# A row sum of 64 MiB: the first two blocks get 17 and 15 rows for each partition, and each its own store

## The chip, the cores and the metric

The kernel runs on one core of a Trainium2 chip. The metric is the device time of one execution in microseconds (us). A profiled execution also has a span, from its first to its last instruction; the time is about 1.8 us more than the span. Times carry noise of a few tenths of a microsecond.

## The reference

```python
# x: float32 [32, 512, 1024]
def reference(x):
    return np.sum(x, axis=-1).astype(np.float32)      # [32, 512]
```

There are 16384 rows of 1024 numbers (4 KiB each), and one sum for each row. With 128 partitions that is 128 rows for each partition, 67.1 MB to read and 64 KiB to write.

## The kernel before

The rows are taken in eight blocks of 16 rows for each partition. Partition p of a block reads 16 neighbouring rows, so neighbouring partitions begin 64 KiB apart in memory. Three buffers rotate. VectorE (DVE) sums whole blocks; ScalarE (ACT) helps in the last two.

```python
    x_g = x.flatten_outer_dims().rearrange("(g p j) d -> g p j d", p=P, j=BIG)     # BIG = 16
    out_v = out.rearrange("b s -> (b s)").rearrange("(g p j) -> p g j", p=P, j=BIG)
    ...
        for g in range(last):                                   # last = 7
            t = inpool.tile([P, BIG * dim + 4], fp32)           # bufs=3
            if g == 0:
                rows(t, 0, FIRST, 0, 0)                         # FIRST = 4: load 4 rows, sum them
                first = sums_of[-1]
                rows(t, FIRST, BIG - FIRST, FIRST, 0)           # load 12, sum them
                continue
            load = rows(t, 0, BIG, g * BIG, BIG // 2 if g == last - 1 else 0)
            ...
        # the last block comes in pieces of 8, 5, 2 rows and two parts of one row
        ...
        hold(store(nc.scalar, 0, last), two, "its packets come behind those of the loads")
        halves(whole[:, :1], part)
        halves(sums[:, j : j + 1], whole)                       # the last sum
        store(nc.sync, last, last + 1)
```

`rows` issues a load on SyncE's queue (SPq in the profile) and the reductions for it. The sums of blocks 0 to 6 leave in one store from ScalarE's queue (ACTq), held until the load `two` has landed (its completion is signalled to the waiting engine); the store writes 128 x 7 = 896 pieces of 16 sums, 64 bytes each. The sums of block 7 leave in a small store from SyncE's queue. Before the closing barrier SyncE waits, in what is called its drain here, for every load and for the ScalarE store. It does not wait there for the last store: GpSimd waits for that one, after the barrier, just before it clears the semaphores.

## Time and profile before

| | before |
|---|---|
| time, median of 3 | 161.64 us (161.48 to 161.78) |
| span of the profiled execution | 159.6 us |
| load queue, share of 16 DMA engines | 97.8% |
| VectorE busy | 120.1 us |
| first load lands | 7.14 us |
| last VectorE sum starts | 157.45 us |
| from there to the end | 2.15 us |

The first landing and the start of the last sum cut the span into a start, a middle and a tail. The prediction shows the lines.

The final store is the last thing in the chain. Its landing at 159.31 releases the clear, and the barrier is done before that. This gives the drain some slack, and one of the two arguments below is about how much.

### The profile page before, as it was taken

The numbers are of one execution on the slowest core, as the hardware profiler recorded it, in microseconds if no ns is written. First come the engines' busy times: TensorE is split into PE (matmuls) and PEld (weight loads), VectorE is DVE, ScalarE is ACT, GpSimd is POOL, SyncE is SP. The second block draws the span as 40 slices with busy tenths as digits, with TensorE's granted clock in tenths as the row PEclk, the third lists the DMA queues.
The fourth block names the chain that finished last, engine by engine and source line by source line (L and its number), as shares of the span: only waits on it lengthen the run. The fifth ranks groups of instructions, "written<-read, shape, count | busy, mean of one in ns | idle before, by whom it ended". The sixth has DMA issues, their size and how long they took to land.

```text
span 159.6 us, 125 instructions
## 1 busy us (share of the span) xinstructions
DVE 120.1 (75%) x22; ACT 17.3 (11%) x31; POOL 0.2 (0%) x4
## 2 busy tenths in 40 slices
DVE  0290059960799958999499994999949999497953
ACT  3000000000000000000000000000000000496953
POOL 0000000000000000000000000000000000000000
DMA  7999996996996989979969969969969969798984
GB/s 263 460 406 579 394 526 263 526 526 263 526 526 263 526 378 411 526 312 476 526 279 509 526 263 526 526 263 526 526 263 526 509 279 526 337 452 371 467 365 128
DMA packets 2928, 67.18 MB, mean 421 GB/s; under 512 B 1264, under 2 KB 1392, under 8 KB 1520
## 3 DMA queue, kind: packets, MB, share of 16 engines
q1 hardware_dynamic: 2016, 67.12, 97.8%
q10 hardware_dynamic: 912, 0.06, 0.4%
HBM read 67.11 MB, written 0.07 MB: 421 GB/s over the span
## 4 chain that ended last, share of the span: by engine, by line
DMA 73%; DVE 25%; SPq 1%; issue 0%; DVEq 0%
DMA t<-in_x_dram 73%; DVE sums L141 24%; SPq L180 1%; SPq L221 0%; DVE t L155 0%; DVEq L252 0%
## 5 line engine op out<-in xcount | busy, mean ns | idle before, releaser
L141 DVE TENSOR_REDUCE sums<-t 128x16 f32<-128x16384 f32 (+3 forms) x9 | 116.6, 12954 | 35.3 <-DMA t<-in_x_dram 35.3
L168 ACT ACTIVATE unread<-t 128x1024 f32<-128x1024 f32 x15 | 15.2, 1012 | 139.2 <-DMA t<-in_x_dram 139.2
L155 DVE CUSTOM_DVE_ANT_0 t<-t 128x512 f32<-128x512 f32 (+2 forms) x6 | 3.5, 602 | 2.4 <-DMA t<-in_x_dram 2.4
L168 ACT ACTIVATION_READ_ACCUMULATOR unread<-t 128x1 f32 x15 | 2.8, 187 | 0.0
L168 ACT ACT_TABLE_LOAD x1 | 1.3, 1283 | 0.8 <-PEq L241 0.8
L155 DVE DVE_READ_ACCUMULATOR2_ANT sums<- 128x1 f32 x5 | 0.4, 83 | 0.0
L241 POOL MEMSET const-uint8-127<- 128x1 uint8 x1 | 0.1, 102 | 0.0
L241 POOL MEMSET const-bfloat16-1.0<- 128x1 bf16 x1 | 0.1, 101 | 0.0
L241 POOL MEMSET const-float32-0.0<- 128x1 f32 x1 | 0.1, 98 | 0.2 <-issue 0.2
L241 POOL MEMSET const-float32-1.0<- 128x1 f32 x1 | 0.1, 98 | 0.0
L155 DVE DVE_READ_ACCUMULATOR2_ANT t<- 128x1 f32 x1 | 0.1, 81 | 0.0
L219 DVE MEMSET t<- 128x1 f32 x1 | 0.1, 59 | 0.0
## 6 DMA issues: line engine op xcount, KB each, us to landing
t<-in_x_dram SPq DMA_DIRECT2D x1, 6144.0 KB, 20.9
t<-in_x_dram SPq DMA_DIRECT2D x1, 4096.0 KB, 31.1
t<-in_x_dram SPq DMA_DIRECT2D x1, 2560.0 KB, 36.9
t<-in_x_dram SPq DMA_DIRECT2D x1, 2048.0 KB, 7.1
t<-in_x_dram SPq DMA_DIRECT2D x1, 1024.0 KB, 38.9
t<-in_x_dram SPq DMA_DIRECT2D x1, 280.0 KB, 39.1
t<-in_x_dram SPq DMA_DIRECT2D x1, 232.0 KB, 39.2
t<-in_x_dram SPq DMA_DIRECT2D x6, 40.8
```

Source lines behind the costliest of these rows:

```text
L141: return nc.vector.tensor_reduce(out=dst, in_=src, axis=mybir.AxisListType.X, op=mybir.AluOpType.add)
L155: return nc.vector.tensor_tensor_reduce(out=src[:, :n], in0=src[:, :n], in1=src[:, n:], scale=1.0, scalar=0.0, op0=mybir.AluOpType.add, op ...
L168: nc.scalar.activation(out=unread[:, :n], in_=src, func=mybir.ActivationFunctionType.Copy, accum_out=dst,)
L180: load = nc.sync.dma_start(out=block, in_=rows_from(j, n))
L219: nc.vector.memset(whole[:, width + 1 :], 0.0)
L241: nc = _bacc.Bacc("TRN2", target_bir_lowering=False, num_devices=1)
```

## The change

The change gives block 0 seventeen rows for each partition and block 1 fifteen. Partitions of block 0 are then 68 KiB apart in memory, not 64. No stated reason came with it; breaking up a power-of-two distance when all engines start together is the likely one. One access pattern no longer describes the outputs of blocks 0 and 1, so each gets its own store. ScalarE now issues three stores where it issued one.

```diff
+    sizes = [BIG + 1, BIG - 1] + [BIG] * (J // BIG - 2)
+    begins = [sum(sizes[:k]) for k in range(len(sizes))]
+    x_b = [
+        x_r[a * P : (a + n) * P].rearrange("(p j) d -> p j d", p=P) for a, n in zip(begins, sizes)
+    ]
+    out_b = [out_r[a * P : (a + n) * P].rearrange("(p j) -> p j", p=P) for a, n in zip(begins, sizes)]
+    out_g = out_r[2 * BIG * P :].rearrange("(g p j) -> p g j", p=P, j=BIG)
     ...
         for g in range(last):
-            t = inpool.tile([P, BIG * dim + 4], fp32)
+            n, j = sizes[g], begins[g]
+            t = inpool.tile([P, (BIG + 1) * dim], fp32)
     ...
-        hold(store(nc.scalar, 0, last), two, "its packets come behind those of the loads")
+        for k in range(2):
+            mine = sums[:, begins[k] : begins[k] + sizes[k]]
+            hold(nc.scalar.dma_start(out=out_b[k], in_=mine), two, behind)
+        middle = sums[:, 2 * BIG : last * BIG].rearrange("p (g j) -> p g j", j=BIG)
+        hold(nc.scalar.dma_start(out=out_g[:, : last - 2], in_=middle), two, behind)
     ...
-        store(nc.sync, last, last + 1)
+        nc.sync.dma_start(out=out_b[last], in_=sums[:, last * BIG :])
```

## The prediction

> **What bounds the kernel now.** I read four views: the page's busy shares and queue table, the merged chain of waits, the timeline of VectorE (DVE), and the stretches of time.
>
> ```profile
> DVE 120.1 (75%) x22; ACT 17.3 (11%) x31; POOL 0.2 (0%) x4
> q1 hardware_dynamic: 2016, 67.12, 97.8%
> ```
>
> VectorE has work for 120.1 of 159.6 us. The load queue's packets cover 97.8% of the span on all 16 DMA engines. The transfers have next to no room.
>
> ```profile
> 7.17 4.42 DVE L141 TENSOR_REDUCE sums<-t 128x4 f32<-128x4096 f32 x1 [7.17 <-DMA t<-in_x_dram]
> 21.67 12.95 DVE L141 TENSOR_REDUCE sums<-t 128x12 f32<-128x12288 f32 x1 [10.08 <-DMA t<-in_x_dram]
> 41.02 17.22 DVE L141 TENSOR_REDUCE sums<-t 128x16 f32<-128x16384 f32 x1 [6.39 <-DMA t<-in_x_dram]
> 60.37 17.22 DVE L141 TENSOR_REDUCE sums<-t 128x16 f32<-128x16384 f32 x1 [2.14 <-DMA t<-in_x_dram]
> 79.76 17.22 DVE L141 TENSOR_REDUCE sums<-t 128x16 f32<-128x16384 f32 x1 [2.17 <-DMA t<-in_x_dram]
> ```
>
> Columns: start, duration, instruction, idle time before it with its releaser. Blocks land every 19.35 us (60.37 - 41.02) and a reduction takes 17.22, so VectorE waits 2.1 us for data at every block. A block is 8.39 MB, so the rate is 8.39/19.35 = 434 GB/s. One row for each partition costs 19.35/16 = 1.209 us of transfer and 17.22/16 = 1.076 us of VectorE.
>
> ```profile
> 0.00:7.14 7.14, 0.00 (x0) 1.28 (x1) 0.20 (x4) 1.00 1.02 404
> 7.14:157.45 150.31, 119.67 (x20) 16.03 (x30) 0.00 (x0) 1.00 0.99 427
> 157.45:159.60 2.15, 0.41 (x2) 0.00 (x0) 0.00 (x0) 1.00 0.18 18
> ```
>
> Columns: stretch, its length, busy time of VectorE, ScalarE and GpSimd, clock, DMA share, GB/s. I cut the span where the first load lands and where the last VectorE sum starts. The middle carries 124 of the 128 rows: 124 x 1.209 = 149.96 of its 150.31 us. It can lose 0.35 us and no more. The first stretch carries 4 rows, 4.84 us of data, in 7.14: 2.3 us are start-up. The last is 2.15 us of a sum, a small store and the closing barrier. So a change in block sizes can act at the two ends only.
>
> **What the Trainium skill says.** "DMA: Bandwidth & Descriptors", section "Bandwidth", "Where 436 GB/s comes from", puts the ceiling at 435 GB/s; the 434 above agrees, so the middle is at it. The same page, "Latency and other measured facts", tells of copies slowing where the row pitch between partitions is a large power of two: 207 GB/s at 512 KiB, 103 at 4 MiB, back to 214 when 4 KiB are added to the pitch. Here a block of 16 rows has a pitch of 64 KiB, and 17 rows make it 68. In the middle this trace shows no such loss; at the start it may (below). That page's "The descriptor swizzle" gives engine = 8 x (partition >> 6) + ((partition >> 2) & 7): neighbouring engines begin four partitions apart, 256 KiB before and 272 KiB after. No view here names the engine of a packet. "SBUF — State Buffer", section "SBUF size: 192, 224, or 256?", leaves about 208 KiB of a partition usable. Three buffers of 17 rows and the sums need 3 x 17 x 4096 + 512 = 209,408 bytes, under 212,992: it fits with three buffers, so nothing is lost there.
>
> **The change part by part.**
>
> 1. *Row counts.* The second piece of block 0 grows from 12 to 13 rows: it lands at 21.67 + 1.21 = 22.9 and is summed in 12.95 + 1.08 = 14.0, ending at 36.9 in place of 34.6. Block 1 has 15 rows and still lands at 41.0, since 31 rows follow the first four or not: the total is unchanged. Its sum takes 16.1, ending at 57.2 rather than 58.2. Everything after is the same. Buffer 0 comes free 2.3 us later, but its next load moves data only from 60.4 (when block 2 has landed), 23 us later; buffer 1 comes free 1 us earlier, in front of a queue that is full anyway. Sum on the path: 0.
>
> 2. *Packets.* In the packet records of the trace a 16 KiB packet takes 611 ns, 48 KiB 1815 and 64 KiB 2418: straight, with about 9 ns for the packet itself. The number of packets (128 for each load) and the bytes stay. Sum: 0.
>
> 3. *The start.* The first 16 packets, one on each engine, start between 1.02 and 1.68 us and take 747 to 1465 ns; later ones of that size take 611. Joining each packet to the one that ends where it starts gives 16 rows of packets, one for each engine; added over its first packets, an engine loses 0.2 to 0.86 us against the 611 pace, and over the remaining 150 us under 0.21 more. So the slow beginning is real and is where a pitch could matter: with 256 KiB between engines all of them begin in the same place modulo every smaller power of two and then drift apart; with 272 KiB they begin 16 KiB apart, just a packet of the first load. But engines share no work, and the last to end sets the time. The one that started last (1.68) lost 0.25 and ended at 156.86, those with the biggest losses at 156.9. If only packet durations improve, the latest starter still holds the end and the gain is under 0.1 us; if the spread of starts is part of the same jam (the store's first packets start within 0.1 us of each other), the ends could come 0.5 us earlier. I take 35% for about 0.45, 20% for about 0.2, the rest for 0: mean 0.2 us gained.
>
> 4. *The end.* One store on ScalarE's queue becomes three. Issue of the old one, from the timeline:
>
> ```profile
> 156.16 0.42 ACTq L191 DMA_DIRECT2D out_dram<-sums  x1
> 157.45 0.40 DVE L155 CUSTOM_DVE_ANT_0 t<-t 128x233 f32<-128x233 f32 x1 [0.16 <-DMA t<-in_x_dram]
> 157.89 0.35 SPq L191 DMA_DIRECT2D out_dram<-sums  x1
> ```
>
> An issue of 896 pieces takes 0.42, one of 128 pieces 0.35. So the three run 156.16 to 156.51, 156.56 to 156.91, and 156.96 to about 157.35. By the packet records the old store's packets began 0.92 after its issue, ran 0.745 for 56 pieces on an engine (13 ns each), and the store landed 0.45 later, at 158.29. The third new store has 40 pieces on an engine: packets from 157.88 to 158.41, landed about 158.86, 0.6 later than now. The final store's packets begin at 158.73, after that, so they should not collide. SyncE drains on the semaphores of these stores before the closing barrier: it now passes its waits by 158.55 and the barrier reaches GpSimd at 158.98, where the clear waits for the final store until 159.31. That is 0.33 us of slack. The new drain comes at about 158.95, the barrier at 159.38: 0.05 to 0.1 us of delay after the slack, plus a wait or two more of 0.07. Sum on the path: +0.05.
>
> Together: 161.64 - 0.2 + 0.05 = 161.49, rounded to **161.5 us**.
>
> **The rivals.**
>
> (a) *Nothing at the start.* The slow first packets are a cold start that any pitch would show. For: the starts are spread already, which a pitch need not cause; the middle runs at full rate at the old pitch; the skill's 512 KiB figure is barely down. Against: 16 first packets end within 0.41 us (2.07 to 2.48) however late they began, as in a queue for one thing. Then only the end is left: 161.7.
>
> (b) *The start is freed entirely.* Starts within 0.2 us and packets at some 750 ns: the first load lands near 6.6 rather than 7.14, and all that follows moves by 0.5: 161.1 to 161.2.
>
> (c) *The end costs more.* If the third store's pieces fall among the final store's, or its landing delays the barrier by all of 0.6 us, the slack is used up and some 0.3 us remain: 161.9 with nothing gained.
>
> (d) *A hole in the loads*, from the later release of buffer 0. The chain speaks against it: a load waits some 40 us between issue and landing, twice a block's 19.35. It would show as VectorE idle over 2.2 us before the reductions at 60 and 80. I give it 2%.
>
> **Range and chances.** The times before span 161.48 to 161.78. From (b) at its best to (c) at its worst gives 161.0 to 161.9. Two per cent is 3.2 us, more than all the start-up (2.3) or the whole tail (2.15), and the middle has 0.35 to give; faster by that needs something that no view shows: 0.5%. Slower needs a failure such as (d) or a full slower transfer at the odd pitch: 1%.
>
> **What the changed profile would show.** Right: the 13-row sum 14.0 us and the 15-row sum 16.1; reductions from the third block on again 2.1 us apart; 434 GB/s in the middle; three ACTq issues ending near 157.35 relative to an unmoved last load; queue q10 still with 912 + 32 = 944 packets. Step 3 is decided by the landing of the first load: 7.14 unchanged means (a), 6.6 means (b). Step 4 by the length from the last sum's start to the end: 2.2 expected, 2.15 no cost, 2.45 rival (c). The prediction is wrong in kind if the middle stretch (first landing to last sum) changes by more than 0.2 us from 150.31, since I say that rows moved between blocks 0 and 1 leave it alone.

## The result, and the profile after

The changed kernel took 162.04 us (median of 6, 161.94 to 162.15), beside 161.66 us (161.48 to 162.12) for the kernel before in the same rounds. The ratio is 1.0022, with a 95% interval of 1.0008 to 1.0036. It is computed from means, the mean time of one kernel's runs over that of the other's in the same rounds, so it is not quite the ratio of the medians. The class "within 2%" was right. The time lies 0.14 us above the predicted range, and its direction was wrong: slower, not faster.

The busy shares and queues of the changed kernel's page, and then VectorE's timeline:

```profile
DVE 120.1 (75%) x22; ACT 17.3 (11%) x31; POOL 0.2 (0%) x4
q1 hardware_dynamic: 2016, 67.12, 97.5%
q10 hardware_dynamic: 944, 0.06, 0.4%
```

```profile
7.47 4.42 DVE L152 TENSOR_REDUCE sums<-t 128x4 f32<-128x4096 f32 x1 [7.47 <-DMA t<-in_x_dram]
23.18 14.02 DVE L152 TENSOR_REDUCE sums<-t 128x13 f32<-128x13312 f32 x1 [11.30 <-DMA t<-in_x_dram]
41.33 16.15 DVE L152 TENSOR_REDUCE sums<-t 128x15 f32<-128x15360 f32 x1 [4.12 <-DMA t<-in_x_dram]
60.68 17.22 DVE L152 TENSOR_REDUCE sums<-t 128x16 f32<-128x16384 f32 x1 [3.20 <-DMA t<-in_x_dram]
80.03 17.22 DVE L152 TENSOR_REDUCE sums<-t 128x16 f32<-128x16384 f32 x1 [2.13 <-DMA t<-in_x_dram]
```

The work is the same 120.1 us and the packets are those expected. The 13-row and 15-row sums take what they should, and from the block at 80 on the wait for data is 2.1 us again. But all starts are 0.3 us later than before, the first one already (7.47 for 7.17); the second is later by one more row's transfer, as foreseen. The stretches, cut as in the prediction at the first landing and at the start of the last sum:

```profile
0.00:7.44 7.44, 0.00 (x0) 1.28 (x1) 0.20 (x4) 1.00 1.01 396
7.44:157.75 150.31, 119.68 (x21) 16.03 (x30) 0.00 (x0) 1.00 0.99 427
157.75:160.24 2.49, 0.41 (x2) 0.00 (x0) 0.00 (x0) 1.00 0.23 23
```

The middle is 150.31 us, as before. The start costs 7.44 - 7.14 = 0.30. The last instruction of the kernel before ends at 159.63, so its tail is 2.18 in full and the new one costs 2.49 - 2.18, 0.32 before rounding. Two losses at the two ends make the whole difference of the spans, 160.24 - 159.63 = 0.62 with the same rounding. The end of the timeline shows the new store issues:

```profile
156.45 0.88 ACTq L232 DMA_DIRECT2D out_dram<-sums  x2
157.37 0.44 ACTq L234 DMA_DIRECT2D out_dram<-sums  x1
157.75 0.40 DVE L166 CUSTOM_DVE_ANT_0 t<-t 128x233 f32<-128x233 f32 x1
158.19 0.35 SPq L237 DMA_DIRECT2D out_dram<-sums  x1
```

The third store is issued at 157.37, 0.92 us after the first. The view of the closing line's instructions, where the columns are the count, the shortest, median and longest duration in ns, and the first and last start, has this for the SyncE queue of the kernel before:

```profile
L252 SPq EVENT_SEMAPHORE  x6: 17/28/28, 158.3 to 159.6; - x6
```

and this for the changed kernel:

```profile
L263 SPq EVENT_SEMAPHORE  x6: 17/28/622, 158.6 to 160.2; - x6
```

No wait of the old drain lasted longer than 28 ns. One wait of the new drain lasts 622 ns, and it is for the third store, which lands at 159.32. The drain, the barrier and the clear come behind it, although the final store it once hid behind had landed at 159.60, before the clear at 159.95.

### The profile page after: what moved, and what is told of

Same layout as the page of the kernel before. It is cut to its first block, busy times and chain, and to the rows that moved or that the text cites. A ratio compares the mean times of both kernels' runs of the same rounds, so it can differ in the third digit from the quotient of the medians.

```text
span 160.2 us, 128 instructions
## 1 busy us (share of the span) xinstructions
DVE 120.1 (75%) x22; ACT 17.3 (11%) x31; POOL 0.2 (0%) x4
## 4 chain that ended last, share of the span: by engine, by line
DMA 74%; DVE 24%; SPq 1%; issue 0%; DVEq 0%
DMA t<-in_x_dram 74%; DVE sums L152 24%; SPq L191 1%; SPq L227 0%; DVE t L166 0%; DVEq L263 0%
## 5 line engine op out<-in xcount | busy, mean ns | idle before, releaser
L152 DVE TENSOR_REDUCE sums<-t 128x16 f32<-128x16384 f32 (+4 forms) x9 | 116.6, 12953 | 35.6 <-DMA t<-in_x_dram 35.6
```

The source lines that it names most:

```text
L152: return nc.vector.tensor_reduce(out=dst, in_=src, axis=mybir.AxisListType.X, op=mybir.AluOpType.add)
```

## The experiments

After the comparison there were two theories to hold against their rivals. For the tail, theory S says that the third ScalarE store lands after SyncE's slack is used up; its rivals are that the row counts cost it, or that the number of stores and waits does. For the start, either the row count of block 0 delays the first landing, or that landing varies from execution to execution.

### The kernel before, again

No edit.

> The kernel before, unchanged, for a second trace and for the noise between runs. If the 0.30 us that the changed kernel loses before the first load lands (7.44 against 7.14 us) belongs to the row counts, this lands at 7.14 again, within 0.1. If that landing merely varies from execution to execution, it may be anywhere from 7.0 to 7.6. The tail, from the start of the last sum to the end, should be 2.15 in any case. Time 161.7, ratio 1.000.

Its first reduction started at 7.16 us (7.17 in the first trace) and its tail was 2.16. Its time was 161.81 us, ratio 1.0009 (0.999 to 1.0028). Its middle, from the start of the first reduction to that of the last sum, was 150.95 us; counted so, the first trace has 150.28. Its times came in two groups, 161.56 to 161.57 and 162.06 to 162.32, and the profiled one was of the slower group. So in this trace some 0.6 us of noise sit in the middle, and the start does not share them.

### Three stores, rows as before

```diff
-        hold(store(nc.scalar, 0, last), two, "its packets come behind those of the loads")
+        for g0, g1 in ((0, 1), (1, 2), (2, last)):
+            hold(store(nc.scalar, g0, g1), two, behind)
```

> All blocks keep 16 rows, only the stores of the changed kernel are taken over: block 0, block 1 and the rest each by itself on ScalarE's queue. Theory S (the third store lands after the slack of SyncE's drain is used up): tail 2.45 to 2.50 as in the changed kernel, ACTq issues 0.4 to 0.5 us apart, time 0.30 to 0.35 us over the kernel before (162.0). Theory R (the row counts cost it, the stores hide): tail 2.15, time 161.7. First landing as in the kernel before under both.

Three parts of the span, cut as above:

```profile
0.00:7.14 7.14, 0.00 (x0) 1.28 (x1) 0.20 (x4) 1.00 1.02 404
7.14:157.50 150.36, 119.67 (x20) 16.04 (x30) 0.00 (x0) 1.00 0.99 427
157.50:160.14 2.64, 0.41 (x2) 0.00 (x0) 0.00 (x0) 1.00 0.22 22
```

The start is that of the kernel before and the tail is even longer than in the changed kernel. One wait of the drain took 766 ns here. The time was 161.95 us, ratio 1.0014 (1.0001 to 1.0027). Theory R, that the row counts cost the tail, has fallen. The late first landing is absent here, so it does not come from the stores.

### The changed kernel with the small stores on SyncE

```diff
-            hold(nc.scalar.dma_start(out=out_b[k], in_=mine), two, behind)
+            hold(nc.sync.dma_start(out=out_b[k], in_=mine), two, behind)
```

> The changed kernel, with the two small stores issued by SyncE, which has nothing to do there, beside the large one on ScalarE's queue. Theory S: the large store lands some 0.9 us earlier than in the changed kernel (about 158.4 on its clock), the drain is back within its slack, tail 2.15 to 2.25; what is left against the kernel before is the start alone: 161.7 if that is chance, 161.95 if the row counts delay the first landing by 0.3. Theory R: as slow as the changed kernel, 162.04.

The end of its timeline, and the waits of its drain:

```profile
156.42 0.82 SPq L232 DMA_DIRECT2D out_dram<-sums  x2
156.43 0.45 ACTq L234 DMA_DIRECT2D out_dram<-sums  x1
157.76 0.40 DVE L166 CUSTOM_DVE_ANT_0 t<-t 128x233 f32<-128x233 f32 x1
158.20 0.33 SPq L237 DMA_DIRECT2D out_dram<-sums  x1
```

```profile
L263 SPq EVENT_SEMAPHORE  x6: 17/28/28, 158.6 to 159.8; - x6
```

Now the large store is issued 0.94 us earlier and lands at 158.44; all early stores have landed by 158.66. No wait is over 28 ns and the tail is 2.15 again. The first landing stays at 7.45. The time was 161.77 us, ratio 1.0008 (0.9993 to 1.0024), against 162.12 for the changed kernel in the same rounds.

### The changed kernel, again

No edit.

> The changed kernel again, for a second trace. Tail 2.45 to 2.50 again. If the row counts delay the first landing, it is 7.4 to 7.5 again and the time 162.04; if it varies from execution to execution, it may be anywhere from 7.0 to 7.6, and the times are spread over 0.3 us or more.

The first reduction started at 7.47 us, the tail was 2.61, and one wait of the drain took 732 ns. The time was 162.12 us, ratio 1.0022 (1.0008 to 1.0036). So both losses repeat.

### Which rows delay the start

The next kernels keep the small stores on SyncE (but where one store is enough) and change the row counts, which set the distance in memory between partitions. Of each edit only the line with the sizes is shown; the views of the output and the stores follow it.

> 15 rows for each partition first and 17 second (pitch 60 KiB in place of 68), small stores on SyncE as in the run before. Theory P (any pitch off the power of two, with engines starting 240 or 272 KiB apart, delays the first packets): first landing 7.4 to 7.5 as with 17 rows. Theory Q (only more rows or a longer second load does): 7.1 to 7.2. Tail 2.15. Time 161.9 under P, 161.6 under Q.

```diff
-    sizes = [BIG + 1, BIG - 1] + [BIG] * (J // BIG - 2)
+    sizes = [BIG - 1, BIG + 1] + [BIG] * (J // BIG - 2)
```

> Block 0 with 16 rows, blocks 1 and 2 with 17 and 15, three small stores on SyncE. If the pitch of the first load is what delays the start, the first landing is 7.16 again as in every trace of 16-row kernels and the time 161.6 to 161.75; if the row counts elsewhere, the changed program or the larger tiles are what matters, it is 7.47. Tail 2.15 to 2.25.

```diff
+    sizes = [BIG, BIG + 1, BIG - 1] + [BIG] * (J // BIG - 3)      # and a third small store
```

> The first load reads one contiguous 2 MiB region (four rows for each partition, pitch 16 KiB, engines 64 KiB apart), the second 12 rows at 48 KiB. Under theory P, where the slow start follows the pitch, this says whether closer engines are better or worse: 7.16 if powers of two are the good case, 7.4 or more if the distance itself matters. Time 161.6 to 161.9 with it. Tail 2.15.

```diff
+    sizes = [4, BIG - 4] + [BIG] * (J // BIG - 1)                 # block 0 is two regions
```

> Blocks 0 and 1 as one region with 32 rows for each partition: pitch 128 KiB, engines 512 KiB apart, one small store of 128-byte pieces. If powers of two are the good case for the start, 7.16 or better and the time 161.6; if a larger distance is worse (a jam in one part of the memory), 7.4 or more in the first landing and perhaps more in the middle stretch than 150.3. Tail 2.15.

```diff
+    sizes = [2 * BIG] + [BIG] * (J // BIG - 2)                    # blocks 0 and 1 are one region
```

> All 128 rows of a partition as one region: pitch 512 KiB, engines 2 MiB apart, one ScalarE store of 448-byte pieces (128 pieces in place of 896). A candidate to beat the kernel before if the start likes large powers of two: first landing 7.1, tail 2.15, time 161.5. If distance makes a jam, as the copies in the skill's table at large pitches, first landing above 7.3 and a middle above 150.3: 162 or more.

```diff
+    sizes = [J]                                                   # all blocks are one region
```

> Blocks 0 to 2 as one region of 48 rows: pitch 192 KiB, no power of two, but engines 768 KiB apart, a multiple of 256 KiB like those of 64 and 128. If what matters is that engines start at the same place modulo 256 KiB, first landing 7.15 to 7.23; if it is the power of two itself, 7.4 or more as with 68. Time 161.65 or 161.95. Tail 2.15 to 2.2.

```diff
+    sizes = [3 * BIG] + [BIG] * (J // BIG - 3)                    # blocks 0 to 2 are one region
```

The kernel with 15 rows first was run a second time, without another edit.

> 15 rows first once more, for a second trace of the start: 7.24 again if the pitch of 60 KiB costs little, 7.4 or more if the first trace was lucky. Tail 2.15. Middle 150.3 or, as in its first trace, 150.9, if that comes and goes from execution to execution.

The start of the first reduction, which is 0.02 to 0.03 us after the first landing, read from VectorE's timeline of each trace, with the number of the chip in brackets ("?" where it is not on record):

| distance between partitions of the first load | kernels | first reduction, us |
|---|---|---|
| 16 KiB | first load compact | 7.62 (11) |
| 60 KiB | 15 first, twice | 7.24 (11), 7.32 (6) |
| 64 KiB | before twice, three stores, odd blocks later | 7.17 (?), 7.16 (15), 7.16 (15), 7.23 (11) |
| 68 KiB | changed kernel twice, small stores on SyncE, large store first (below) | 7.47 (?), 7.47 (15), 7.48 (15), 7.59 (6) |
| 128 KiB | blocks 0 and 1 one region | 7.14 (11) |
| 192 KiB | blocks 0 to 2 one region | 7.38 (6) |
| 512 KiB | all blocks one region | 7.57 (6) |

The chips must be kept apart. The same distance started later on chip 6: 60 KiB by 0.08 us against chip 11, 68 KiB by 0.11 to 0.12 against chip 15. Whether that is the chip or chance, a difference of 0.1 between chips says nothing here.

The kernel with 16 rows in block 0 and 17 and 15 in blocks 1 and 2 has all else of the change, the larger tiles and the odd blocks included:

```profile
7.23 4.42 DVE L152 TENSOR_REDUCE sums<-t 128x4 f32<-128x4096 f32 x1 [7.23 <-DMA t<-in_x_dram]
21.76 12.95 DVE L152 TENSOR_REDUCE sums<-t 128x12 f32<-128x12288 f32 x1 [10.11 <-DMA t<-in_x_dram]
```

Its start is back with those of the kernel before. So the row count of the block that is read first delays the start. Four traces with 64 KiB and four with 68 do not overlap, and on chip 15 alone they are 7.16 twice against 7.47 and 7.48. The kernels of 128 and 16 KiB, both on chip 11 and with 12 rows in the second load as before, show that the distance can move the landing without a longer second load:

```profile
7.14 4.42 DVE L152 TENSOR_REDUCE sums<-t 128x4 f32<-128x4096 f32 x1 [7.14 <-DMA t<-in_x_dram]
7.62 4.42 DVE L152 TENSOR_REDUCE sums<-t 128x4 f32<-128x4096 f32 x1 [7.62 <-DMA t<-in_x_dram]
```

For 68 KiB itself one rival stands. Its four traces all have 13 rows in the second load too, and 15 rows first, with 11 there, came out near theory Q (7.24, where Q had 7.1 to 7.2 and P 7.4 to 7.5). No run has 13 rows in the second load at 64 KiB, so distance and second load are not separated there.

The rules that I tried against the table fail. "Powers of two are good" fails at 512 and 16. "A distance between engines that is a multiple of 256 KiB is good" fails at 512 (7.57, beside 7.32 for 60 KiB on the same chip); 192 KiB, at 7.38 between the two values that its expectation named and without a trace of 64 KiB on its chip, decides nothing. "Any step off 64 is bad" fails at 128. "Apart is better", the idea behind my prediction, fails at 68. The distances with one trace are weak evidence each, and the second trace of 60 KiB (7.32) fell between its two expected values too; which part of the memory the engines meet in was not seen.

In times these kernels tell little. 15 rows first took 161.95 and 161.75 us in its two runs (ratios 1.0003 and 1.001), odd blocks later 161.69 (0.9996), 128 KiB 161.60 (0.9984, interval 0.9956 to 1.0013), 192 KiB 161.72 (1.0012) and 512 KiB 161.98 (1.0019); all intervals reach 1. No version beats the kernel before by more than noise.

The compact first load was clearly slower: 162.85 us, ratio 1.0059 (1.0031 to 1.0088). Its start explains 0.45 of it. Its tail was 3.28 us, because two of its stores landed late (count, size and us from issue to landing):

```profile
out_dram<-sums ACTq DMA_DIRECT2D x1, 48.0 KB, 3.4
out_dram<-sums SPq DMA_DIRECT2D x1, 2.0 KB, 1.7
out_dram<-sums SPq DMA_DIRECT2D x1, 6.0 KB, 3.3
out_dram<-sums SPq DMA_DIRECT2D x1, 8.0 KB, 2.1
```

The 6 KB store writes pieces of 48 bytes, the 2 KB store, which was not late, pieces of 16. By the trace's packet records the packets of these three early stores had all ended by 158.19, while the two late landings came at 160.01 and 160.22: the delay lies between the last packet and the landing.

### The same three stores, the large one first

The three stores are the same; the lines of the large one are moved up, and their removal below is not shown.

```diff
+        middle = ...
+        hold(nc.scalar.dma_start(out=out_g[:, : last - 2], in_=middle), two, behind)
         for k in range(2):
             mine = sums[:, begins[k] : begins[k] + sizes[k]]
             hold(nc.scalar.dma_start(out=out_b[k], in_=mine), two, behind)
```

> The changed kernel with the same three stores on ScalarE's queue, the large one first and the small ones behind it. Theory S (landing of the last store against the drain's slack): the last one now has 8 pieces on an engine, not 40, so it lands 0.4 us earlier, tail 2.15 to 2.25, time 161.75. Theory N (the number of stores and of waits in the drain): tail 2.5 to 2.6 as before, time 162.04. First landing 7.47 under both.

The tail was 2.25 us. The longest wait of the drain fell to 380 ns:

```profile
L263 SPq EVENT_SEMAPHORE  x6: 17/28/380, 158.7 to 160.1; - x6
```

Three stores and all their waits are there, so theory N, the number of stores, has fallen: the tail follows the landing of the last one. The time was 161.84 us (ratio 1.0009, 0.9989 to 1.0029). With the semaphore times of the traces (when each transfer's completion was signalled) this can be put in one table, each landing counted from the start of the last sum, in us:

| kernel | last early store lands | final store lands | tail |
|---|---|---|---|
| before | 0.84 | 1.86 | 2.18 |
| small stores on SyncE | 0.90 | 1.84 | 2.15 |
| large store first | 1.33 | 1.86 | 2.25 |
| changed | 1.57 | 1.85 | 2.50 |
| changed, again | 1.68 | 1.86 | 2.61 |
| three stores, rows as before | 1.71 | 1.88 | 2.64 |

In the last four lines the tail is the early landing plus 0.93 (0.92 by the rounded figures of the first of them). In the first two it is the final landing plus 0.31 (0.32 by the rounded figures of the first). The two meet where the early landing is at 1.86 + 0.31 - 0.93 = 1.24, so the kernel before had a slack of 1.24 - 0.84 = 0.40 us. The constant 0.93 is good to about 0.05 only: outside the table it was 0.88 with odd blocks later (early landing 1.33, tail 2.21, with four early stores) and 0.95 with the compact first load (2.33 and 3.28).

## Why the prediction was wrong

**What bounds the kernel, and steps 1 and 2** were right. The middle was 150.31 us before and after. The later release of buffer 0 cost nothing, and rival (d) did not happen. The 13-row sum took 14.02 and the 15-row sum 16.15 us, and q10 has the 944 packets foreseen. One thing is left out there: the section that the prediction cites for 435 GB/s also says that the HBM side, about 358 GB/s, binds transfers between HBM and SBUF. The 434 GB/s measured here, with one core at work, lies above that, so of the section's figures the 435 is the one that fits.

**Step 3, "mean 0.2 us gained", failed**, and so did its widest case for and against: I had the start between no gain and a gain of 0.5 us, and gave a loss there no part of the sum (a slower transfer at the odd pitch stood only among the 1% for a change of 2%). The first landing came 0.30 us later in the trace, and the four traces of each kind repeat it. In the packet records (the start and duration of every DMA packet) of the changed kernel the first 16 packets start between 1.01 and 1.92 us and take 719 to 1578 ns. An engine loses 0.67 us on average to slow first packets (0.59 before), so the average is worse only by about a tenth. The landing waits for the last of the 16 engines, which ended at 7.10 rather than 6.79. Over the four traces of each kind the averages overlap (0.55 to 0.74 us lost with 68 KiB, 0.55 to 0.59 with 64), but the last engine ended at 7.10 to 7.24 with 68 and 6.78 to 6.83 with 64. I had seen that the slowest engine decides, but let the new distance only help it. That the distance can move the landing is shown (7.14 to 7.62 on one chip); how it acts, and whether at 68 KiB it or the longer second load does, is open. Rival (a), a cold start that any pitch would show, is also wrong, since the landing moved with the pitch by half a microsecond.

**Step 4, "Sum on the path: +0.05", had the right mechanism and the wrong size.** It measured +0.32 in the first trace of the changed kernel and 0.43 and 0.46 in the two other traces with three stores in this order. The sum was short by its own terms already: 0.05 to 0.1 and 0.07 make 0.12 to 0.17, and only 0.05 was carried on. (The 0.07 for more waits did not come: the closing line has six SyncE semaphore instructions before and after.) Beyond that, two terms were small. I put the landing of the third store at 158.86, which is 2.70 us after the first issue; it was 2.86, mostly because the issues stood 0.49 and 0.43 us apart where I had taken 0.40. And I counted 0.52 us from that landing to the barrier's reaching GpSimd (159.38 - 158.86), and 0.31 more to the end as after the final store's landing before, 0.83 in all; 0.93 were needed. Together 0.26, and they fall on the path in full, since the slack was used up already: with the 0.07 by which the predicted barrier (159.38) was later than the final landing (159.31) they make the 0.32 measured, to 0.01. Rival (c) named 2.45 us as the mark of this and was closest; the pieces of the stores did not collide, though, and it was its other half, the late barrier, that came true.

**The sum.** The traces give 0.30 + 0.00 + 0.32 = 0.62 us, as do the times of the two profiled executions (161.40 and 162.02). The medians differ by 0.38 only. The likely part of the reason is on the other side: of the 37 timed executions of the kernel before in all rounds, 14 took 161.8 us or more, up to 162.32, and the profiled one of these had a middle of 150.95. The changed kernel's 12 all took 161.94 to 162.15, so the slower kind, which also came in kernels of odd rows with the small stores on SyncE, was not seen among them. Why it was not stays open.

## What to carry to other kernels

Where a stream of transfers is at the engines' rate, moving rows between its first two blocks cost nothing here (the middle stayed at 150.31 us), and the change acted at the two ends: work these out in tenths of a microsecond, from the landing times. A store that is hidden behind a later one has a slack; splitting it on one queue adds an issue time of 0.4 to 0.6 us for each store, and the last landing, not the number of stores, then sets the end, so put the largest first or use an idle queue. The distance in memory between partitions moved the start of the first sum between 7.14 and 7.62 us on one chip. Against the 64 KiB of the kernel before the gain was 0.09 us at most and the loss up to 0.39 there, and none of the rules tried explains it, so it should be tried rather than reasoned.

## What the Trainium skill lacked or had wrong

- "DMA: Bandwidth & Descriptors", "Latency and other measured facts", tells of row pitch as a matter of a long copy's rate and starts its table at 512 KiB. Here the steady rate of the one kernel with all blocks at 512 KiB was that of 64 KiB (a block in 19.34 us, 60.69 to 80.03, beside 19.35), but the first landing followed the pitch: 7.14 us (128 KiB), 7.16 to 7.23 (64), 7.24 and 7.32 (60), 7.38 (192), 7.47 to 7.59 (68), 7.57 (512), 7.62 (16), for the start of the first reduction, over three chips, between which the same distance differs by up to 0.12. Padding by 4 KiB, which it advises for its large pitches, came with a start 0.3 us later at 64.
- The same page, "Issuing engines are not separate DMA queues", calls the time to issue usually small beside the transfer. For stores of about 8 KB at the end of this kernel it was a quarter to a third of the time to landing (0.39 to 0.55 us of 1.5 to 2.0), and it was on the path: issues on ScalarE's queue stood 0.43 to 0.58 us apart, and moving two of three to SyncE took the tail from 2.50 to 2.15 us.
- No page gives the landing time of small stores by the size of their pieces: stores of 128 pieces took 1.4 to 1.6 us with 64 bytes, 1.5 with 128 and 192, and 1.5 to 2.2 with 60 and 68. In the one run with pieces of 16 and 48 bytes they took 1.7 and 3.3, and the two stores beside them were late too (3.4 and 2.1 us for 48 KB and 8 KB in pieces of 64 bytes; 2.1 and 1.4 for 56 KB and 8 KB in the kernel before).
